# Regrouping the transposes and scores of a GLA and MLP layer, and cutting its first step by columns

## The chip, the cores and the metric

The kernel runs on one core of a Trainium2 chip. The metric is the device time of one execution, in microseconds (us). Before the change it is 1073.5 us, the median of three runs (1072.7, 1073.5 and 1073.9).

## The reference, cut to what matters

The layer takes 256 tokens of width 2048. It is a chunk-causal gated linear attention followed by a squared-ReLU MLP, each with a residual, and a final RMSNorm:

```
proj = rmsnorm(x) @ w_in              # q 1024, k 1024, v 2048, r 2048, g_low 16 columns
log_a = log_sigmoid(g_low @ w_gate_up + b_gate) / 16
# 4 heads, chunks of 64 tokens: the state decays per chunk, o = q_c @ state
h = x + (rmsnorm_per_head(o) * o_norm * silu(r)) @ w_out
a = relu(rmsnorm(h) @ w_up)           # 2048 -> 8192
h = h + (a * a) @ w_down              # 8192 -> 2048
out = rmsnorm(h)
```

Everything is float32 to the outside.

## The kernel before, in words

**Products.** A float32 product is made of three float32r matmuls. Each operand is split into a high part (rounded to float32r) and a low part (the rest), and the kernel adds high by high, high by low and low by high. `weights` (L119) loads a strip of 128 rows of a weight matrix with the SP queue into a `raw` buffer; `parts` (L105) makes the high part with a ScalarE cast (L109) and the low part with a VectorE subtraction (L110). There are five pairs of `hi`/`lo` buffers and six half buffers of `raw`, so casts run some steps ahead of TensorE. TensorE works with a stationary operand of 128x128 that is loaded anew for every matmul (the PEld rows) and a moving operand of 256 columns, or 272 in the first projection.

**Two forms of projection.** `natural` (L153) computes tokens by columns: 16 steps, one for each 128 rows (`kt`) of the contraction, each with 24 matmuls: two token tiles `t`, three terms, up to 1024 columns as halves of 256. The stationary operand is a row tile of activations given by the function `row`, the moving one the weights. `turned` (L168) computes columns by tokens, with the weights stationary: 16 values of `kt`, 12 matmuls each, loaded two `kt` at a time (`kp`). After each step (`natural`) or each `kt` (`turned`) but the last, `pump` (L88) takes one entry from the queue `side`; what is left at the end of a stage `flush` runs. So `side` spreads other work over the steps, and an entry `nothing` leaves a step empty. The position is not binding: the planner puts each instruction on its engine when its own timing model finds it ready, with the order of the program as the priority. Inside `pump`, `issue_after` only keeps an entry's ScalarE and VectorE work behind the latest cast.

**The stages, in order.** (1) The value and gate projection (`w_vg`, 1040 columns, L324). While it runs, `input_tile` (L248) loads x in six pieces and makes its high part `xh` (ScalarE, L255) and low part `xl` (VectorE, L256) for each `kt`; for the first three steps (`FINE`) the weights are loaded and cast in two pieces of columns. (2) The keys, two `turned` halves, with the gate's 22 entries in `side`, each followed by `nothing`: `turn_gate` (L343, two transposes), `gate_logits`, exponentials, scans. (3) The queries, two `turned` halves. (4) The second half of the values (`natural`, L480), with `scores` (L448): per head, three groups of plain float32 matmuls (12 records on TensorE) into two `aux` banks, evacuated by four ScalarE and four VectorE instructions. (5) The first half of the r projection (L533), with `attend`. (6) Its second half (L551), and (7), (8) the two halves of the output projection (L572, L579), with `turn` (L520): transposes of `on`, later of `h`, by plain float32 matmuls against `ident`, two `kt` (four transposes) at a time into one `aux` bank, then two ScalarE and two VectorE instructions that make the split parts. The last four of these calls run in the first `turned` stage of the MLP (`up`, L614), before the scale of the second norm (`scale2`, `scale2_row`). (9) Four rounds of `up` and `down`, and the end. PSUM is six `acc` banks and two `aux` banks.

**The operand at another address.** All stationary operands start 48 columns past a multiple of 64 columns (`OFF`). A few steps use one that starts at a multiple of 64 instead: `xe` (a copy of the row tile of `kt` 5, `t` 0, made in L260 and L261) in `row_x`; `row_o` for `kt` 5, `t` 0; and, in `turned`, the second `kt` of the pairs listed in `even`. `even_at` (L148) moves step `EVEN` (5) to another place in the order. These steps are called resets below.

**What follows a stage.** `put_v` (L317), `gate_out` (L512) and `add_h` (L559) read the four `acc` banks of a finished `natural`, two column halves `c` for each of two token tiles `t`, with `t` as the outer loop.

Of the kernel before, what the change touches and what calls it, by code (L numbers as in the profile page):

```python
# [32 lines left out]
P = 128  # L33
T = 256
# [32 lines left out]
def tile_gla_mlp(ctx, tc, x, xt, cols, w_vg, w_in, w_gate, w_out, w_up, w_down, final_norm, out):  # L67
# [14 lines left out]
    def aux_bank():  # L82
        return aux_p.tile([P, 512], F32, tag="aux", name="aux")
# [21 lines left out]
    def parts(raw, n, to, pieces=None):  # L105

        hi, lo = to
        for s in (slice(*p) for p in pieces or [(0, n)]):
            last_hi[0] = nc.scalar.copy(hi[:, s], raw[:, s])  # L109
            last_lo[0] = nc.vector.tensor_tensor(lo[:, s], raw[:, s], hi[:, s].bitcast(F32), op=ALU.subtract)  # L110
        return hi, lo
# [7 lines left out]
    def weights(src, n, pieces=None, room=None, skip=0, raw=None, gap=None):  # L119


        to = room or slots()
        if raw is None:
            if not raw_half:
                raw_half.extend(raw_pair())
            raw = raw_half.pop(0)
        for s in (slice(*p) for p in pieces or [(0, n)]):
            dst = raw[:, s]
            if len(src.shape) == 3:
                dst = dst.rearrange("p (i c) -> p i c", i=2)  # L130
                last_load[0] = nc.sync.dma_start(out=dst, in_=src)
                between = SLOT - OFF - 2 * GT if gap else 0
                to = [a[:, OFF - between : OFF + 2 * GT + between].rearrange("p (i c) -> p i c", i=2)[:, :, between:] for a in to]
                last_hi[0] = nc.scalar.copy(to[0], dst)  # L134
                last_lo[0] = nc.vector.tensor_tensor(to[1], dst, to[0].bitcast(F32), op=ALU.subtract)  # L135
                return to
            else:
                last_load[0] = nc.sync.dma_start(out=dst, in_=src[:, s])  # L138
        return parts(raw, n, to, pieces or [(skip, n)])

    def halves(o, x, w, first, last):

# [10 lines left out]
    def natural(row, source, n, cuts, pumps=1, ahead=None, order=range(KT)):  # L153

        acc = acc_banks(NT * len(cuts))
        acc = [acc[t * len(cuts) : (t + 1) * len(cuts)] for t in range(NT)]
        for step, kt in enumerate(order):
            wh, wl = weights(source(kt), n, ahead and ahead(kt))
            for t in range(NT):
                sh, sl = row(kt, t)  # L160
                for i, (s, w) in enumerate(((sh, wh), (sh, wl), (sl, wh))):
                    for c, (lo, hi) in enumerate(cuts):
                        halves(acc[t][c], s, w[:, lo:hi], step == 0 and i == 0, step == KT - 1 and i == 2)
            if step < KT - 1:
                pump(pumps)
        return acc
# [23 lines left out]
    def rows(w, c0, n=G, r0=0):  # L190
        return lambda kt: w[r0 + kt * P : r0 + (kt + 1) * P, c0 : c0 + n]
# [31 lines left out]

    xe = mid.tile([P, 2, P], F32R, tag="xe", name="xe")

    def row_x(kt, t):
        if kt == EVEN and t == 0:
            return [xe[:, i] for i in range(2)]
        return [a[:, kt, t * P : (t + 1) * P] for a in (xth, xtl)]

    def wrap_input(lo, hi):
        k = slice(lo, hi)
# [15 lines left out]
    def input_tile(kt):  # L248
        if kt in x_loads:
            s = slice(x_done[0], x_loads[kt])  # L250
            nc.sync.dma_start(out=xr[:, s, :], in_=xv[:, s, :])  # L251
            x_done[0] = x_loads[kt]
        if kt == KT - 1:
            wrap_input(0, KT - 2)
        nc.scalar.activation(xth[:, kt, :T], xr[:, kt, :], AF.Copy, scale=g1(kt))  # L255
        nc.vector.scalar_tensor_tensor(  # L256
            xtl[:, kt, :T], xr[:, kt, :], g1(kt), xth[:, kt, :T].bitcast(F32), op0=ALU.mult, op1=ALU.subtract
        )
        if kt == EVEN:
            nc.scalar.copy(xe[:, 0], xth[:, kt, :P].bitcast(F32))  # L260
            nc.vector.tensor_copy(xe[:, 1], xtl[:, kt, :P].bitcast(F32))  # L261
        return [(0, 512), (512, WMAX)] if kt < FINE else None


    h = const.tile([P, NT, D], F32, name="h")

    GR = 64 + RANK
# [53 lines left out]
            vh[:, t, c0 : c0 + n].bitcast(F32), op0=ALU.mult, op1=ALU.subtract,  # L321
        )

    acc = natural(row_x, rows(w_vg, 0, WMAX), WMAX, cuts, ahead=input_tile)  # L324
    flush()
    wrap_input(KT - 2, KT)
    for t in range(NT):
# [76 lines left out]
    gate += [lambda c=c: gate_scan(c) for c in range(8)]  # L404
    gate += [lambda i=i: gate_spans(i) for i in range(2)]
    gate += [gate_spans_even, gate_decays, gate_decays_even]
    for g in gate:
        side.extend([g, nothing])

# [5 lines left out]
        nc.vector.tensor_tensor(kab[:, 0, c], kab[:, 0, c], zz[:, 1, c], op=ALU.mult)  # L415

    for half in range(2):
        acc = turned(*xts, w_in, KEYW + half * GT, even=(0,) if half else (2,), acc=None if half else [aux_bank(), aux_bank()])
        for b in range(2):
            c0 = 4 * half + 2 * b  # L420
            from_bank(kab[:, 0, c0 : c0 + 2], acc[b])
# [88 lines left out]
    oth = otl = None  # L510

    def gate_out(acc, c0):  # L512
        for t in range(NT):
            for c in range(2):
                lo = c0 + 512 * c
                s = tmp.tile([P, 512], F32, tag="t512", name="sr", bufs=3)
                nc.scalar.activation(s, acc[t][c], AF.Silu, scale=r1[:, t : t + 1])
                nc.vector.tensor_tensor(on[:, t, lo : lo + 512], on[:, t, lo : lo + 512], s, op=ALU.mult)

    def turn(src, row, gain, q):  # L520
        b = aux_bank()
        for i in range(2):
            kt = 2 * q + i
            for t in range(NT):
                nc.tensor.transpose(b[:, i * T + t * P : i * T + (t + 1) * P], src[:, t, kt * P : (kt + 1) * P], ident)  # L525
        for i in range(2):
            kt = 2 * q + i
            s = b[:, i * T : (i + 1) * T].rearrange("p (t s) -> p t s", t=NT)
# [30 lines left out]
    def add_h(acc, c0):  # L559
        for t in range(NT):  # L560
            for c in range(2):
# [258 lines left out]
```

## Time and profile before

| what | value |
|---|---|
| median of three runs | 1073.5 us (1072.7 to 1073.9) |
| the profiled execution's own time | 1072.98 us |
| its span, first to last instruction | 1071.1 us |
| TensorE (PE) busy | 1061.8 us, 99%, 9283 matmul records |
| VectorE (DVE) busy | 775.1 us, 72% |
| ScalarE (ACT) busy | 574.2 us, 54% |
| GpSimd (POOL) busy | 12.7 us, 1% |
| read from HBM | 206.92 MB, 195 GB/s over the span |

The profile is one execution taken by the hardware profiler. PE rows are matmuls, PEld rows the loads of the stationary operand, which overlap them. Matmuls are pipelined, so a record is longer than the distance between the starts of two neighbours; that distance (the pitch) is what TensorE's time consists of, and it is read from the start times in the timeline. A row of a timeline holds its start, its length, the engine and line, the operation with the tiles it writes and reads, the shape and the number of records in it. What stands in brackets is idle time before it and who ended it.

### The profile page before, as it was taken

The page shows a single profiled execution, that of the slowest core. Times are in us where ns is not written, and L with a number is a line of the kernel's source. Part 1 is how long each engine was busy: PE and PEld are TensorE (multiplying, and loading weights), DVE is VectorE, ACT ScalarE, POOL GpSimd, SP SyncE. Part 2 cuts the span into 40 slices and gives each one's busy share as a digit, 9 for nine tenths or more (in the row PEclk, how much of TensorE's full clock was granted, in tenths as well). Part 3 has the DMA queues.
Part 4 walks back from the last instruction along what each step waited for, and adds up shares of the span by engine and source line. Part 5 has one row for each costly group of instructions (what it writes and reads, how often), then busy time and mean ns, then how long its engine had stood idle before and what let it go on. Part 6 is the DMA issues. An engine that isn't in the chain of part 4 may idle for free.

```text
span 1071.1 us, 21851 instructions
## 1 busy us (share of the span) xinstructions
PE 1061.8 (99%) x9283; PEld 1060.9 (99%) x9283; DVE 775.1 (72%) x1026; ACT 574.2 (54%) x693; POOL 12.7 (1%) x39
## 2 busy tenths in 40 slices
PE   9999999999999999999999999999999999999997
PEld 9999999999999999999999999999999999999997
DVE  7677654656555566789986689987779997678874
ACT  7675444546445455555555446564555554555552
POOL 0000000000000000000000000000000000000000
PEclk9999999999999999999999999999999999999999
DMA  9847654655555555555576555566655656665662
GB/s 341 305 157 233 196 185 137 178 151 179 197 183 183 186 179 183 194 190 201 197 227 204 191 194 173 195 223 210 197 197 179 213 200 215 191 194 189 205 228 79
DMA packets 79569, 210.43 MB, mean 196 GB/s; under 512 B 6720, under 2 KB 7616, under 8 KB 79344
## 3 DMA queue, kind: packets, MB, share of 16 engines
q1 hardware_dynamic: 78512, 206.99, 58.6%
q10 hardware_dynamic: 960, 2.05, 0.5%
q8 instruction: 72, 1.18, 0.4%
q14 instruction: 25, 0.20, 0.1%
HBM read 206.92 MB, written 2.10 MB: 195 GB/s over the span
## 4 chain that ended last, share of the span: by engine, by line
PE 96%; DMA 1%; issue 1%; ACT 0%; DVE 0%; SPq 0%; POOLq 0%; POOL 0%; DVEq 0%; ACTq 0%
PE acc L146 42%; PE acc L180 39%; PE aux L146 12%; PE aux L180 2%; DMA zz<-in_xt 1%; PE aux L525 1%; PE aux L454 1%; DMA raw<-in_w_vg 0%; ACT xh L255 0%; SPq L138 0%; DVE lo L110 0%; ACT hi L109 0%; PE acc L355 0%; SPq L251 0%; DVE hf L779 0%
## 5 line engine op out<-in xcount | busy, mean ns | idle before, releaser
L110 DVE TENSOR_TENSOR lo<-raw,hi 128x1024 fp32r<-128x1024 f32 (+2 forms) x225 | 258.5, 1151 | 123.2 <-ACT hi L109 122.2
L109 ACT CAST hi<-raw 128x1024 fp32r<-128x1024 f32 (+2 forms) x225 | 223.4, 994 | 214.9 <-PE acc L146 115.5
L180 PE MATMUL acc<-hh,hi 128*128 128x256 f32 x1024 | 283.2, 277 | 0.0
L180 PE MATMUL acc<-hh,lo 128*128 128x256 f32 x1024 | 283.1, 276 | 0.0
L180 PE MATMUL acc<-hl,hi 128*128 128x256 f32 x1024 | 283.0, 276 | 0.0
L135 DVE TENSOR_TENSOR lo<-raw,hi 128x1024 fp32r<-128x1024 f32 x160 | 195.7, 1224 | 115.3 <-ACT hi L134 114.6
L134 ACT CAST hi<-raw 128x1024 fp32r<-128x1024 f32 x160 | 168.1, 1051 | 187.5 <-PE acc L180 144.7
L146 PE MATMUL acc<-hi,act 128*128 128x256 f32 x1202 | 217.3, 276 | 0.0
L180 PEld LDWEIGHTS acc<-hh,hi 128*128 128x128 f32 x1024 | 192.3, 188 | 0.0
L180 PEld LDWEIGHTS acc<-hh,lo 128*128 128x128 f32 x1024 | 192.3, 188 | 0.0
L180 PEld LDWEIGHTS acc<-hl,hi 128*128 128x128 f32 x1024 | 192.3, 188 | 0.0
L146 PEld LDWEIGHTS acc<-hi,act 128*128 128x128 f32 x1202 | 180.2, 188 | 0.0
L146 PE MATMUL acc<-lo,act 128*128 128x256 f32 x601 | 142.1, 276 | 0.0
L146 PE MATMUL aux<-hi,act 128*128 128x256 f32 x716 | 135.1, 276 | 0.0
L146 PEld LDWEIGHTS aux<-hi,act 128*128 128x128 f32 x716 | 107.9, 188 | 0.0
L146 PEld LDWEIGHTS acc<-lo,act 128*128 128x128 f32 x601 | 101.9, 188 | 0.0
L146 PE MATMUL acc<-lo,xh 128*128 128x256 f32 x496 | 79.7, 279 | 0.1
L146 PE MATMUL acc<-hi,xh 128*128 128x256 f32 x496 | 78.7, 281 | 0.3 <-ACT hi L109 0.3
L146 PE MATMUL acc<-hi,xl 128*128 128x256 f32 x496 | 78.8, 278 | 0.0
L146 PE MATMUL aux<-lo,act 128*128 128x256 f32 x358 | 76.9, 276 | 0.0
L109 ACT CAST hi<-work 128x1024 fp32r<-128x1024 f32 x49 | 51.7, 1055 | 32.0 <-PE aux L146 12.0
L146 PEld LDWEIGHTS acc<-hi,xh 128*128 128x128 f32 x496 | 66.7, 188 | 0.8 <-ACT hi L109 0.7
(147 smaller groups left out, 1386.1 us busy)
## 6 DMA issues: line engine op xcount, KB each, us to landing
raw<-in_w_up SPq DMA_DIRECT2D x128, 512.0 KB, 4.5
raw<-in_w_down SPq DMA_DIRECT2D x128, 512.0 KB, 4.4
raw<-in_w_in SPq DMA_DIRECT2D x80, 512.0 KB, 4.6
raw<-in_w_out SPq DMA_DIRECT2D x32, 512.0 KB, 4.3
raw<-in_w_vg SPq DMA_DIRECT2D x13, 520.0 KB, 8.0
h<-in_x SPq DMA_DIRECT2D x4, 512.0 KB, 7.1
zz<-in_xt SPq DMA_DIRECT2D x3, 384.0 KB, 7.5
fb<-in_final_norm ACTq DMA_DIRECT2D x1, 1024.0 KB, 7.0
```

The lines of the kernel that those rows point to most:

```text
L109: last_hi[0] = nc.scalar.copy(hi[:, s], raw[:, s])
L110: last_lo[0] = nc.vector.tensor_tensor(lo[:, s], raw[:, s], hi[:, s].bitcast(F32), op=ALU.subtract)
L134: last_hi[0] = nc.scalar.copy(to[0], dst)
L135: last_lo[0] = nc.vector.tensor_tensor(to[1], dst, to[0].bitcast(F32), op=ALU.subtract)
L146: nc.tensor.matmul(o[:, m], x, w[:, m], start=first and c == 0, stop=last, skip_group_check=True)
L180: nc.tensor.matmul(o, u[:, i, s], m[:, kt], start=kt == 0 and n == 0 and j % 2 == 0, stop=kt == KT - 1 and n == 2, skip_group_check=True,)
L454: nc.tensor.matmul(o, kab[:, k[0], c0 + c, k[1] : k[1] + P], q(qt[:, c0 + c]), start=c == 0, stop=c == 1)
L525: nc.tensor.transpose(b[:, i * T + t * P : i * T + (t + 1) * P], src[:, t, kt * P : (kt + 1) * P], ident)
```

## The change

It makes these edits.

- `turn` handles four `kt` (eight transposes) into two `aux` banks in a call. `turns` puts two such calls into a stage, each after an entry `nothing`: after steps 1 and 3 of stages 6, 7 and 8; in the first `up` stage each entry has one more `nothing` behind it.
- `scores` entries get a `nothing` after each and three instead of one ahead; the gate's entries get five `nothing` ahead. Counting the queue through the stages, the four heads come after steps 8, 10, 12 and 14 of stage 4 (before: after 5, 6, 7 and 8), and `turn_gate` after `kt` 5 of the keys (before: after `kt` 0).
- Both value projections take `plain_x`, without the reset; the second one has the plain order of steps.
- Resets in `turned` move: the first half of the keys from pair 2 to pair 4, the first `up` from pair 5 to pair 6.
- In the first step of the first projection the products go by pieces of columns: for each of 512, 256 and 272 columns first high by high for both token tiles, then high weights by low x, then low weights by high x. The weights of the first two `kt` (before: three) are loaded in two pieces and cast in three.
- From `kt` 3 on, the split of x (`split_input`) is kept behind the casts of the previous step's weights, on ScalarE and on VectorE.
- `gate_out` and `add_h` go over columns first, then token tiles.

```diff
-        for s in (slice(*p) for p in pieces or [(0, n)]):
+        loads, pieces = pieces or ([(0, n)], [(skip, n)])
+        for s in (slice(*p) for p in loads):
...
-        return parts(raw, n, to, pieces or [(skip, n)])
+        return parts(raw, n, to, pieces)
...
+            terms = lambda t: [(row(kt, t)[x], (wh, wl)[y]) for x, y in ((0, 0), (0, 1), (1, 0))]
+            if ahead and step == 0:
+                for c, (lo, hi) in enumerate(cuts):
+                    for i in (0, 2, 1):
+                        for t in range(NT):
+                            s, w = terms(t)[i]
+                            halves(acc[t][c], s, w[:, lo:hi], i == 0, False)
+            else:
...
+    def plain_x(kt, t):
+        return [a[:, kt, t * P : (t + 1) * P] for a in (xth, xtl)]
...
+        with ExitStack() as order:
+            if kt >= FINE:
+                order.enter_context(tc.issue_after(last_hi[0].ins))
+                order.enter_context(tc.issue_after(last_lo[0].ins))
+            split_input(kt)
+        return ([(0, 512), (512, WMAX)], [(0, 256), (256, 512), (512, WMAX)]) if kt < 2 else None
...
-        return [(0, 512), (512, WMAX)] if kt < FINE else None
...
-    acc = natural(row_x, rows(w_vg, 0, WMAX), WMAX, cuts, ahead=input_tile)
+    acc = natural(plain_x, rows(w_vg, 0, WMAX), WMAX, cuts, ahead=input_tile)
...
+    side.extend([nothing] * 5)
     for g in gate:
         side.extend([g, nothing])
...
-        acc = turned(*xts, w_in, KEYW + half * GT, even=(0,) if half else (2,), acc=None if half else [aux_bank(), aux_bank()])
+        acc = turned(*xts, w_in, KEYW + half * GT, even=(0,) if half else (4,), acc=None if half else [aux_bank(), aux_bank()])
...
-    side.extend([lambda: None] + [lambda hd=hd: scores(hd) for hd in range(HEADS)])
-    acc = natural(row_x, rows(w_in, 3 * KEYW), G, HALF, order=even_at(11))
+    side.extend([nothing] * 3 + [f for hd in range(HEADS) for f in (lambda hd=hd: scores(hd), nothing)])
+    acc = natural(plain_x, rows(w_in, 3 * KEYW), G, HALF)
...
-        for t in range(NT):
-            for c in range(2):
+        for c in range(2):
+            for t in range(NT):
...
     def turn(src, row, gain, q):
-        b = aux_bank()
-        for i in range(2):
-            kt = 2 * q + i
+        bs = [aux_bank(), aux_bank()]
+        for i in range(4):
+            kt, b, o = 4 * q + i, bs[i // 2], i % 2 * T
             for t in range(NT):
-                nc.tensor.transpose(b[:, i * T + t * P : i * T + (t + 1) * P], src[:, t, kt * P : (kt + 1) * P], ident)
+                nc.tensor.transpose(b[:, o + t * P : o + (t + 1) * P], src[:, t, kt * P : (kt + 1) * P], ident)
...
-    side.extend([lambda: None] + [lambda q=q: turn(on, turned_o, gain_o, q) for q in range(4)])
+    def turns(src, row, gain, q0):
+        return [f for q in (q0, q0 + 1) for f in (nothing, lambda q=q: turn(src, row, gain, q))]
+    side.extend(turns(on, turned_o, gain_o, 0))
...
-    side.extend([lambda q=q: turn(on, turned_o, gain_o, q) for q in range(4, 8)])
+    side.extend(turns(on, turned_o, gain_o, 2))
...
-    side.extend([lambda: None] + [lambda q=q: turn(h, turned_h, g2, q) for q in range(4)])
+    side.extend(turns(h, turned_h, g2, 0))
...
-    side.extend([lambda q=q: turn(h, turned_h, g2, q) for q in range(4, 8)])
+    side.extend([f for g in turns(h, turned_h, g2, 2) for f in (g, nothing)])
...
-        acc = turned(hth, htl, w_up, r * D + q * GT, even=() if q > 1 or r > 0 and q else (5,) if r == q == 0 else (0,))
+        acc = turned(hth, htl, w_up, r * D + q * GT, even=() if q > 1 or r > 0 and q else (6,) if r == q == 0 else (0,))
```

More of the change, by code (lines that the diff above doesn't have):

```diff
@@ L158, in natural @@
             wh, wl = weights(source(kt), n, ahead and ahead(kt))
-            for t in range(NT):
[L160 to L163, printed above, removed]
+            terms = lambda t: [(row(kt, t)[x], (wh, wl)[y]) for x, y in ((0, 0), (0, 1), (1, 0))]
[7 more added lines that the diff above has]
+                for t in range(NT):
+                    for i, (s, w) in enumerate(terms(t)):
+                        for c, (lo, hi) in enumerate(cuts):
+                            halves(acc[t][c], s, w[:, lo:hi], step == 0 and i == 0, step == KT - 1 and i == 2)
             if step < KT - 1:
@@ L224, in tile_gla_mlp @@
     xe = mid.tile([P, 2, P], F32R, tag="xe", name="xe")
+    def plain_x(kt, t):
+        return [a[:, kt, t * P : (t + 1) * P] for a in (xth, xtl)]
     def row_x(kt, t):
-        if kt == EVEN and t == 0:
-            return [xe[:, i] for i in range(2)]
-        return [a[:, kt, t * P : (t + 1) * P] for a in (xth, xtl)]
+        return [xe[:, i] for i in range(2)] if (kt, t) == (EVEN, 0) else plain_x(kt, t)
     def wrap_input(lo, hi):
@@ L252, in input_tile, with split_input @@
             x_done[0] = x_loads[kt]
+        with ExitStack() as order:
[4 more added lines that the diff above has]
+        return ([(0, 512), (512, WMAX)], [(0, 256), (256, 512), (512, WMAX)]) if kt < 2 else None
+    def split_input(kt):
         if kt == KT - 1:
@@ L512, in gate_out @@
     def gate_out(acc, c0):
-        for t in range(NT):
-            for c in range(2):
+        for c in range(2):
+            for t in range(NT):
                 lo = c0 + 512 * c
@@ L520, in turn @@
     def turn(src, row, gain, q):
-        b = aux_bank()
-        for i in range(2):
-            kt = 2 * q + i
+        bs = [aux_bank(), aux_bank()]
+        for i in range(4):
+            kt, b, o = 4 * q + i, bs[i // 2], i % 2 * T
             for t in range(NT):
-                nc.tensor.transpose(b[:, i * T + t * P : i * T + (t + 1) * P], src[:, t, kt * P : (kt + 1) * P], ident)
-        for i in range(2):
-            kt = 2 * q + i
-            s = b[:, i * T : (i + 1) * T].rearrange("p (t s) -> p t s", t=NT)
+                nc.tensor.transpose(b[:, o + t * P : o + (t + 1) * P], src[:, t, kt * P : (kt + 1) * P], ident)
+        for i in range(4):
+            kt, b, o = 4 * q + i, bs[i // 2], i % 2 * T
+            s = b[:, o : o + T].rearrange("p (t s) -> p t s", t=NT)
             dh, dl = row(kt)
@@ L553, in tile_gla_mlp @@
     gate_out(acc, G)
-    side.extend([lambda q=q: turn(on, turned_o, gain_o, q) for q in range(4, 8)])
+    side.extend(turns(on, turned_o, gain_o, 2))
     hs = const.tile([P, NT, 4], F32, name="hs")
     def add_h(acc, c0):
-        for t in range(NT):
-            for c in range(2):
+        for c in range(2):
+            for t in range(NT):
                 lo = c0 + 512 * c
```

## The prediction

> **What bounds the kernel now.** I read the page first (busy shares, then the chain that ended last), then TensorE's timeline step by step, then ScalarE's where TensorE idles. From the page:
>
> ```profile
> PE 1061.8 (99%) x9283; PEld 1060.9 (99%) x9283; DVE 775.1 (72%) x1026; ACT 574.2 (54%) x693; POOL 12.7 (1%) x39
> PE 96%; DMA 1%; issue 1%; ACT 0%; DVE 0%; SPq 0%; POOLq 0%; POOL 0%; DVEq 0%; ACTq 0%
> ```
>
> TensorE bounds it nearly everywhere, so a gain must come from its idle time or its pitch. The pitch has two values. By the windows, 4412 records take 500 us between 560 and 1060 us: 113.3 ns each. Around the scores and the next stage's reset TensorE's timeline (start, length, what, records) shows:
>
> ```profile
> 156.22 0.62 PE L146 MATMUL acc<-lo,xh 128*128 128x256 f32 x4
> 156.68 0.62 PE L146 MATMUL acc<-hi,xl 128*128 128x256 f32 x4
> 157.13 1.70 PE L454 MATMUL aux<-qt,kab 128*128 128x128 f32 x12
> 158.59 0.72 PE L146 MATMUL acc<-hi,xh 128*128 128x256 f32 x4
> 159.15 0.63 PE L146 MATMUL acc<-lo,xh 128*128 128x256 f32 x4
> 159.62 0.63 PE L146 MATMUL acc<-hi,xl 128*128 128x256 f32 x4
> ...
> 186.41 0.63 PE L146 MATMUL acc<-lo,xh 128*128 128x256 f32 x4
> ...
> 191.12 0.63 PE L146 MATMUL acc<-hi,xl 128*128 128x256 f32 x4
> 191.59 0.64 PE L146 MATMUL acc<-hi,xe 128*128 128x256 f32 x4
> ...
> 193.02 0.62 PE L146 MATMUL acc<-hi,xh 128*128 128x256 f32 x4
> ```
>
> Four matmuls take 0.455 us before the group of scores and 0.47 us after it: from 186.41 to 191.12 us 40 take 4.71 us, 117.7 ns each. The reset (`xe`, 12 matmuls in 1.43 us) ends that, and the next stage runs at 113.3. The reset of this stage itself, at 177.43 us, was followed by 117.7 as before. So a plain float32 group costs 4.4 ns on every matmul up to the next reset that works. Of seven resets met in the slow state, five worked (59.5, 191.6, 259, 350.8, 398 us) and two didn't (20.1 and 177.4, in the two value projections). Once, at 298.4 us, a group of transposes itself brought 113.3 back.
>
> The start, where TensorE waits:
>
> ```profile
> 4.69 0.80 PE L146 MATMUL acc<-hi,xh 128*128 128x256 f32 x2
> 5.77 0.54 PE L146 MATMUL acc<-hi,xh 128*128 128x256 f32 x2 [0.28 <-ACT hi L109]
> 6.14 0.40 PE L146 MATMUL acc<-lo,xh 128*128 128x256 f32 x2
> ...
> 8.54 1.12 PE L146 MATMUL acc<-hi,xh 128*128 128x256 f32 x8
> ```
>
> The first step's 24 matmuls last from 4.69 to 8.54 us, 3.85 us, where step 1 needs 2.86. Its second pair waits for the second piece of weights, cast at 5.09. Then, around 23 us, from ScalarE and TensorE:
>
> ```profile
> 18.77 2.91 ACT L255 ACTIVATE xh<-zz,colt 128x256 fp32r<-128x256 f32 x7 [2.68 <-DMA zz<-in_xt]
> 21.86 1.06 ACT L109 CAST hi<-raw 128x1040 fp32r<-128x1040 f32 x1
> ...
> 22.97 1.22 PE L146 MATMUL acc<-hi,xh 128*128 128x256 f32 x8
> 24.25 0.75 PE L146 MATMUL acc<-lo,xh 128*128 128x256 f32 x4
> ```
>
> Seven splits of x, for steps 9 to 15, run ahead of the cast of step 6's weights, which had landed at 20.09 us. Four pitches there are too long: 45, 102, 219 and 106 ns, 0.47 us in all.
>
> **The change part by part.** The profiled execution took 1072.98 us (span 1071.1 and 1.9 around it), 0.5 below the median of 1073.5; the sum is made against 1072.98, and the 0.5 is added at the end.
>
> *First step by columns.* A 512-column cast takes 0.62 us; 256-wide splits follow each other every 0.40. So the first piece is ready about 0.2 us earlier and TensorE starts at 4.49. From the first 512 columns it now has 12 matmuls (`xl` ready at 4.54, both `lo` pieces by 5.5) before it needs the cast that ends at 5.72. But until about 6 us it isn't at full speed: the warm-up records stand 213 ns apart, the transposes of the same 128 columns later 109. At some 230 ns a matmul (between those 213 and the 254 read at 5.77) about 7 instead of 3 have begun by 6.03. I take 4 x 0.118 = 0.47 us gained. Ends: 1.0 gained, since step 1 can start no sooner than 7.5 (its weights are cast from 7.08); 0.3 lost, if the new order waits for a `lo` piece. By the Trainium skill ("TensorE: Matmul & The Clock Gate", section "What's actually happening") the clock opens after a free-running window of about 3.4 us of work. By that rule it could open anywhere from 4.5 to 7.9 us, and I estimate 1.05 to 0.37 us for this step; the trace agrees: the full pitch is read from 6.03 us, 5.0 us after the first matmul.
>
> *Loads of the third `kt` in one piece.* One SP issue fewer (0.43 us) and one cast fewer on each engine; the whole 520 KB must land (9.22 us) before the 1.06 us cast, ending at 10.3, with `lo` at 11.5. Step 2 starts near 10.95 and wants `lo` near 11.4: 0 to 0.15 us lost; I take 0, as the planner already moves ready products ahead.
>
> *Splits of x behind the casts.* From `kt` 3 each split waits for the previous step's cast; step `kt` needs its own cast anyway, which comes later. Per step ScalarE has 0.4 + 1.06 and VectorE 0.4 + 1.24 us of work in 2.88. Step 6's cast can then run at 20.1 to 21.2 and its `lo` to 22.4, for a step that starts at 22.5; step 7's weights land at 22.19 and are ready at 24.5, for 25.4. Gain 0.47; ends 0 and 0.47, nothing else stood there. ScalarE's block on the three `wgu` issues up to 18.73 us stays.
>
> *Keys.* `turn_gate` comes after `kt` 5 and the reset at `kt` 9 instead of 5: 48 matmuls more at 4.4 ns, 0.21 lost. The gate's later entries move five `kt`; they feed VectorE and ScalarE work needed two stages later. If this reset fails, the next is eight `kt` on: 0.4.
>
> *Second values.* The scores start after step 8 instead of 5: 72 matmuls leave the slow pitch, 0.32 gained; the lost reset didn't work and its 12 matmuls ran at 120: 0.03 gained. The last head now sits one step before the end, so its evacuation (2.9 us for head 0) stands before `put_v`. The next stage needs its third bank 1.4 us after it starts; before, that bank was free 1.1 us earlier: 0 to 0.3 lost, I take 0.
>
> *Transposes.* Their number stays. A group of four costs 445 ns beside its neighbours, so about 111 each; only the edge is saved when two groups merge, 9 ns: 0.07 in all. In stages 6 and 8 the slow stretch is as before (from after step 1 to step 5). In stage 7 it begins a step later but lacks the lucky return at 298.4: 84 instead of 64 matmuls, 0.09 lost. In `up` it is `kt` 3 to 13 instead of 1 to 11: nothing. The two banks of one call are evacuated while the stage runs (see the rivals). `gate_out` and `add_h`: the banks that the next stage needs first, 1.4 us after its start, are still read among the first two or three: nothing.
>
> Sum: -0.47 - 0.47 + 0.21 - 0.35 - 0.07 + 0.09 = -1.06 us: 1071.9, and 1072.4 beside the median.
>
> The resets rest on a pitch that depends on where the stationary operand starts. The Trainium skill speaks against it ("TensorE: Matmul & The Clock Gate", section "Step-by-step: what each phase is for"): loading the next weights doesn't steal read bandwidth from the running matmul. By that rule the moves of groups and resets would be worth nothing and the sum -1.0. The trace disagrees: same shapes, 113.3, 117.7 and 119 ns.
>
> **The rivals.**
>
> - *A, the start gives less.* The first step stays bound by its data and the stall reappears one step later: -0.2 in place of -0.94, 1073.1. For it: loads land one after another up to 18 us with the DMA engines fully busy. Against: the cast of step 6 waited for ScalarE, not for its load.
> - *B, a reset fails.* Dearest is the one at the start of the r projection, now only one step behind a group; 177.43 failed 6 matmuls behind one. Then that stage and five steps of the next, 21 x 24 matmuls, run at 117.7: 2.2 us, 1074.6. A failure at step 5 of stages 6 to 8 costs about 13 steps: 1.4, 1073.8. For it: two of seven failed. Against: the reset at the same place worked.
> - *C, a group brings the fast pitch back*, as at 298.4, in two of the five stretches: with 4 steps each some 0.4, or 0.7 in the values; or resets as before and the start's upper end (0.5 more): 1070.9. For it: one case in some eighteen groups. Against: all the others.
> - *D, the other side: the second turn of a stage comes too late.* A call now holds both banks. Before, two `kt` took from 249.14 to 252.71 us to evacuate, as ScalarE and VectorE alternate on one bank with a cast between: 3.6, so up to 7.1 for four, while the next call is due 5.6 after the transposes: 1.5 us late. That is inside step 4, ahead of the reset. From 2.8 us late on, it falls behind the reset of step 5, and 13 steps of the next stretch run slow: 1.4 us in each of three stages, 4.2 in all, 1076.6. If TensorE waits instead, 1.5 in each of four stages: 1078. Against: the two banks can be evacuated side by side, four pairs of 0.47 + 0.48 being 3.8.
> - *E, nothing moves*: the splits weren't the cause and the step is clock-bound: 1073.5 with the phase terms.
>
> **How the numbers follow.** Forecast 0.47 (own range 1071.4 to 1073.2), A and E 0.13, B 0.15, C 0.13, D 0.12. The bound for a change that can be told from none, about 0.2%, lies at 1071.35 and 1075.65. Forecast, A, E and B are inside, less some 0.02 of the forecast that falls below, and some 0.01 of B, two failures, above: same 0.72. C gives faster 0.15 with that rest; D and double failures slower 0.13. The range runs from C's middle (1070.6, the start's upper end with it) to 1075.5, which takes in all but half of C and D.
>
> **What would show it.** The first step shorter than 3.6 us, from about 4.5; splits of x and casts alternating on ScalarE up to 20 us, and no pitch over 150 ns at 22 to 25; the slow pitch from 66 us back instead of 61, and in the values only from 165; eight transposes as one row of 0.9 us; the fast pitch after each reset. Wrong would be: 117.7 lasting past a reset by a stage (B), idle time ahead of transposes or transposes after step 5 (D), or 113.3 right after a group (C).

## The result, and the profile after

The changed kernel takes 1075.39 us, the median of 20 executions (1074.87 to 1075.91), against 1073.16 for the kernel before in the same comparison (20 executions, 1072.56 to 1074.88). The ratio is 1.0019, with a 95% interval of 1.0013 to 1.0025: 2.2 us slower. The forecast was 1.1 us faster than the 1073.5 shown. The executions of the kernel before lie in two clusters (over all comparisons of this document 95 of 118 below 1074.0 and 23 between 1074.1 and 1075.1), which is why its range is so wide.

The profiled execution of the changed kernel took 1075.38 us, with a span of 1073.2 (1071.1 before). On its page the busy line of section 1 and the chain that ended last read:

```profile
PE 1064.2 (99%) x9283; PEld 1063.6 (99%) x9283; DVE 774.9 (72%) x1027; ACT 574.4 (54%) x694; POOL 12.8 (1%) x39
...
PE 98%; issue 1%; DMA 0%; SPq 0%; DVE 0%; ACT 0%; POOLq 0%; POOL 0%; DVEq 0%
```

TensorE has the same 9283 matmuls and is busy 2.4 us longer, and its share of the chain rose from 96% to 98% as that of DMA fell from 1% to 0%. So waits went away, and the matmuls themselves became slower. Where that happened is seen by the start of each stage's first matmul in the two traces:

| stage | before, us | after, us | difference | forecast |
|---|---|---|---|---|
| start and first projection (to its end) | 52.19 | 51.35 | -0.84 | -0.94 |
| keys, first half | 23.26 | 23.83 | +0.57 | +0.21 |
| keys, second half, and queries | 65.36 | 65.40 | +0.04 | 0 |
| second values (4) | 50.78 | 50.44 | -0.34 | -0.35 |
| r, first half (5) | 51.75 | 51.75 | 0 | 0 |
| r, second half (6) | 45.67 | 46.81 | +1.14 | -0.02 |
| output, first half (7) | 45.59 | 45.87 | +0.28 | +0.07 |
| output, second half (8) | 45.68 | 46.80 | +1.12 | -0.02 |
| first `up` | 24.57 | 24.72 | +0.15 | -0.02 |
| the rest, to the end | 666.20 | 666.26 | +0.06 | 0 |
| sum | 1071.06 | 1073.24 | +2.18 | -1.06 |

(The -0.07 for the edges of groups stands here divided over the four stages, and rounded.) Nearly the whole loss sits in stages 6 and 8. The view by windows shows it as fewer matmuls begun in the same time. Its columns are the window, its length, and then busy time and records of PE, PEld, DVE, ACT and POOL, TensorE's granted clock, the DMA share and GB/s. The kernel before:

```profile
248.00:300.00 52.00, 52.00 (x457) 52.00 (x456) 29.84 (x35) 26.75 (x35) 0.00 (x0) 1.00 0.56 183
335.00:380.00 45.00, 45.00 (x396) 45.00 (x396) 24.64 (x29) 22.32 (x33) 0.00 (x0) 1.00 0.56 188
```

The changed kernel:

```profile
60.00:74.00 14.00, 14.00 (x121) 14.00 (x119) 8.15 (x11) 8.17 (x13) 0.00 (x0) 1.00 0.57 192
248.00:300.00 52.00, 52.00 (x445) 52.00 (x444) 29.11 (x34) 25.93 (x34) 0.00 (x0) 1.00 0.57 183
335.00:380.00 45.00, 45.00 (x387) 45.00 (x386) 24.30 (x27) 21.77 (x32) 0.00 (x0) 1.00 0.54 182
```

TensorE is busy for the whole of each window and has the full granted clock (1.00), in both kernels, yet it begins 12 and 9 matmuls fewer in the last two (the kernel before has 126 in the first window, 5 more). Times 113 ns that is 1.4, 1.0 and 0.6 us. In the timeline of the changed kernel (start, length, engine and line, operation and tiles, shape, records) stage 6 shows why:

```profile
254.76 1.04 PE L541 MATMUL aux<-ident,on 128*128 128x128 f32 x8
...
258.46 0.65 PE L147 MATMUL acc<-hi,xe 128*128 128x256 f32 x4
...
259.90 0.63 PE L147 MATMUL acc<-hi,xh 128*128 128x256 f32 x4
260.38 0.63 PE L147 MATMUL acc<-lo,xh 128*128 128x256 f32 x4
260.85 0.63 PE L147 MATMUL acc<-hi,xl 128*128 128x256 f32 x4
```

Eight transposes, one step (24 matmuls) without side work, then the reset (`xe`, three rows, of which the first is shown). Behind it the rows start 0.47 to 0.48 us apart, that is 117.7 ns per matmul, as ahead of it: this reset fails. In the kernel before, the last group of this stage (four transposes) lay inside the reset, behind its first matmul:

```profile
258.59 0.28 PE L146 MATMUL acc<-hi,xe 128*128 128x256 f32 x1
258.71 0.60 PE L525 MATMUL aux<-ident,on 128*128 128x128 f32 x4
259.06 0.60 PE L146 MATMUL acc<-hi,xe 128*128 128x256 f32 x3
```

In stage 8 it lay behind the reset's second matmul (350.09, in a reset from 349.85). Both resets worked there. So the resets of stages 6 and 8 kept their step, but the last group moved from inside the reset to 24 matmuls ahead of it.

In the changed kernel the slow pitch lasts through stage 6 into stage 7, whose own reset, with the same eight transposes at the same distance, works:

```profile
305.47 0.64 PE L147 MATMUL acc<-hi,oth 128*128 128x256 f32 x4
...
306.90 0.62 PE L147 MATMUL acc<-hi,oth 128*128 128x256 f32 x4
307.35 0.62 PE L147 MATMUL acc<-lo,oth 128*128 128x256 f32 x4
```

From 306.90 on four matmuls take 0.45. In stage 8 the reset at 351.13 fails like that of stage 6, and the slow pitch lasts until the reset of the first `up` stage. In the keys the reset at `kt` 9 fails too; the gate's matmuls (L369) lie inside it and, two more at 65.97, right behind it:

```profile
65.01 0.40 PE L369 MATMUL acc<-gt,wgs 80*128 80x256 f32 x2
```

What was forecast for the start and the values is there. ScalarE alternates between splits of x and casts near 20 us, and the cast of step 6's weights, at 21.86 before, now waits for its load alone:

```profile
20.41 1.06 ACT L109 CAST hi<-raw 128x1040 fp32r<-128x1040 f32 x1 [0.91 <-DMA raw<-in_w_vg]
```

So TensorE no longer stalls at 22 to 25 us; four matmuls take 0.48 there, two rows of which are:

```profile
22.57 1.12 PE L147 MATMUL acc<-hi,xh 128*128 128x256 f32 x8
23.53 0.64 PE L147 MATMUL acc<-lo,xh 128*128 128x256 f32 x4
```

And the last scores, at 186.66 one step ahead of the next stage's reset at 191.02, did that reset no harm; behind it four matmuls take 0.46:

```profile
192.45 0.62 PE L147 MATMUL acc<-hi,xh 128*128 128x256 f32 x4
192.91 0.62 PE L147 MATMUL acc<-lo,xh 128*128 128x256 f32 x4
```

### The profile page after: what moved, and what is told of

Read it like the earlier page. It is cut to its first block, busy times and chain, and to the rows that moved or that the text cites. A ratio compares the mean times of both kernels' runs of the same rounds, so it can differ in the third digit from the quotient of the medians.

```text
span 1073.2 us, 21853 instructions
## 1 busy us (share of the span) xinstructions
PE 1064.2 (99%) x9283; PEld 1063.6 (99%) x9283; DVE 774.9 (72%) x1027; ACT 574.4 (54%) x694; POOL 12.8 (1%) x39
## 4 chain that ended last, share of the span: by engine, by line
PE 98%; issue 1%; DMA 0%; SPq 0%; DVE 0%; ACT 0%; POOLq 0%; POOL 0%; DVEq 0%
PE acc L147 43%; PE acc L188 39%; PE aux L147 12%; PE aux L188 2%; PE aux L541 1%; PE aux L469 1%; DMA raw<-in_w_vg 0%; SPq L139 0%; PE acc L369 0%; SPq L260 0%; DVE hf L798 0%; ACT sqf L751 0%; DVE h L658 0%; ACT hi L109 0%; POOLq L835 0%
## 5 line engine op out<-in xcount | busy, mean ns | idle before, releaser
L110 DVE TENSOR_TENSOR lo<-raw,hi 128x1024 fp32r<-128x1024 f32 (+3 forms) x226 | 258.8, 1147 | 131.3 <-ACT hi L109 130.3
L109 ACT CAST hi<-raw 128x1024 fp32r<-128x1024 f32 (+3 forms) x226 | 223.3, 990 | 226.9 <-PE acc L147 128.1
L147 PEld LDWEIGHTS acc<-lo,xh 128*128 128x128 f32 x504 | 68.1, 188 | 0.0
```

What stands on the lines that cost most here:

```text
L147: nc.tensor.matmul(o[:, m], x, w[:, m], start=first and c == 0, stop=last, skip_group_check=True)
```

## The experiments

The first theory is rival B of the prediction: the start and the scores gained what was forecast, and the loss is that resets fail. What makes them fail was open: how the groups lie (theory 1), what came before (rival 2), their nearness (rival 3). Each kernel below was timed against the kernel before on the same chip; a profile of each gives the lengths of the stages.

**One part undone or alone.** Two kernels keep one part alone, and two put one back.

`start_alone`, the kernel before with the hunks of `weights`, of `natural`'s first step and of `input_tile`:

```diff
+            if ahead and step == 0:
+                for c, (lo, hi) in enumerate(cuts):
...
+            split_input(kt)
+        return ([(0, 512), (512, WMAX)], [(0, 256), (256, 512), (512, WMAX)]) if kt < 2 else None
...
```

> Edit: the kernel before with the edits of the start alone (first step by pieces of columns, third weights in one piece, splits of x behind the casts). Theory 1 (the start gained what the trace shows and the loss lies only in resets that fail): the second stage begins 0.84 us earlier than before, every later stage keeps its length, 1072.3 against 1073.2. Rival (the gain is given back later, because weights or buffers are late where TensorE is ahead): between 1073.0 and 1073.4, with some later stage longer by as much.

Measured: 1072.90 against 1073.20, ratio 0.9995 (0.9987 to 1.0004). The keys begin at 51.83 instead of 52.19, only 0.36 earlier, and their first half takes 23.81 instead of 23.26: their reset, at its old place, fails here. All later stages keep their length within 0.07. The expected 1072.3 is missed by that failure, and the time alone can't be told from that of the kernel before. So no wait for data gives the start back later, but the outcome of a reset that no edit touched has changed. Its surroundings did change: the gate's transposes, at 57.73 and 59.26 ahead of the reset (from 59.48) in the kernel before, lie inside it here (59.50 and 60.20, in a reset from 58.91 to 60.43). Why the start itself gained less than in the changed kernel is told below.

`four`, the changed kernel with the transposes as before:

```diff
-    side.extend(turns(on, turned_o, gain_o, 0))
+    side.extend([lambda: None] + [lambda q=q: turn(on, turned_o, gain_o, q) for q in range(4)])
...
-        bs = [aux_bank(), aux_bank()]
-        for i in range(4):
+        b = aux_bank()
+        for i in range(2):
...
```

> Edit: the changed kernel with the old calls of four transposes, each after steps 1 to 4 (0 to 3 in stage 7), the old reset of the first up stage and the old loop order behind a stage. Theory 1 (how the groups lie decides whether the reset at step 5 works): the resets at about 258 and 350 us work again, stages 6 and 8 are 1.1 us shorter each, stage 7 0.3 shorter: 1072.9 against 1075.4 for the changed kernel. Rival 2 (what the scores or the start left behind decides it): both resets still fail, 1075.2 or so.

Measured: 1072.43, ratio 0.9990 (0.9981 to 0.9999), 2.96 below the changed kernel. Stages 6, 7 and 8 take 45.47, 45.59 and 45.68. In stage 6 the second group of four itself brings the fast pitch back, which is rival C, one time in this stage:

```profile
251.76 0.60 PE L540 MATMUL aux<-ident,on 128*128 128x128 f32 x4
...
252.66 0.62 PE L147 MATMUL acc<-lo,xh 128*128 128x256 f32 x4
253.11 0.62 PE L147 MATMUL acc<-hi,xl 128*128 128x256 f32 x4
```

So the calls of the transposes (or the loop order and the reset of `up` that go back with them) carry the loss; the start and the scores, still in this kernel, don't.

`keys_back`, the changed kernel with the old place of the gate's entries and of the keys' reset:

```diff
-    side.extend([nothing] * 5)
...
-        acc = turned(*xts, w_in, KEYW + half * GT, even=(0,) if half else (4,), ...
+        acc = turned(*xts, w_in, KEYW + half * GT, even=(0,) if half else (2,), ...
```

> Edit: the changed kernel with the gate's entries and the reset of the first half of the keys back where they were (transposes after the first kt, reset in the third pair). Theory 1 (the reset at kt 9 failed, and the slow pitch lasted a stage): first half of the keys 23.3 instead of 23.8 us, 1074.85. Rival (the half is longer because of something else, such as the gate's work in it): no shorter, 1075.4.

Measured: 1073.59, 1.80 below the changed kernel, not 0.55. The first half of the keys takes 23.25, as expected. But stage 6 is 45.67 as well: its reset works, almost 200 us after that of the keys, with the same eight transposes at the same distance. (Without the five empty entries the queue runs ahead: the scores come a step earlier; `attend` lies where it did.) Stage 8 still fails, 46.80. So the outcome hangs on more than where the group lies.

`turns_alone`, the kernel before with the edits of `turn`, `turns`, the moved reset of `up` and the loop order:

```diff
-    side.extend([lambda: None] + [lambda q=q: turn(on, turned_o, gain_o, q) for q in range(4)])
+    side.extend(turns(on, turned_o, gain_o, 0))
...
-        acc = turned(hth, htl, w_up, ... else (5,) if r == q == 0 else (0,))
+        acc = turned(hth, htl, w_up, ... else (6,) if r == q == 0 else (0,))
```

> Edit: the kernel before with the edits of the transposes alone (eight a call, two steps apart, the moved reset of the first up stage, the loop order behind a stage). Theory 1 (the loss sits in how these groups lie to the resets, and whether one fails hangs on what came before it): at least one of the resets at 258 and 350 us fails, 1.1 us or more lost, 1074.2 to 1075.4. Rival 2 (what the start and the scores left behind made them fail): neither fails, 1073.2.

Measured: 1074.59 against 1073.19, ratio 1.0013 (1.0004 to 1.0022): slower by 1.40. Stage 6 works (45.67), stage 8 fails (46.80), and the `up` stage behind it takes 24.72 instead of 24.57. By the stages this one failure costs 1.12 + 0.15 = 1.27, near the 1.4 at which the prediction priced it; stage 7 is 0.08 longer (45.67), as it lacks the lucky return, and the start of this execution 0.22.

**What the failing reset needs.** Six kernels keep all of the change and disturb one thing near the reset of step 5.

`one_more` and `two_more` put one or two matmuls with an all-zero moving operand ahead of the step, in stages 6 and 8; `one_more_stage7` puts one in stage 7 alone:

```diff
+            if kt == EVEN:
+                for _ in range(more):
+                    halves(acc[1][1][:, :T], row(kt, 1)[0], zero, False, False)
...
-    acc = natural(row_x, rows(w_in, 5 * KEYW), G, HALF)
+    acc = natural(row_x, rows(w_in, 5 * KEYW), G, HALF, more=1)
```

> Edit: the changed kernel with one more float32r matmul (an all-zero moving operand, so the sum stays the same) right ahead of the reset's step in stages 6 and 8. Theory 1a (the slow state has a phase that moves with every matmul, and the reset works from some of them): the resets at 258 and 350 us come out differently, that is they work: 1.1 us less in each stage, 0.24 for the two matmuls: 1073.1. Theory 1b (the phase is set by the groups alone and stays from one matmul to the next): the resets fail as before, 1075.6. A reset that works after one and fails after two would be 1a.

> Edit: as with one extra all-zero matmul ahead of the reset's step in stages 6 and 8, but two. Theory 1a with a phase that alternates from one matmul to the next: both resets fail as without any, stages 6 and 8 of 47.05 us, 1075.6. Theory 1a with a longer period, or a rival in which any interruption of the step order heals the reset: both work, stages of 45.9, 1073.2.

> Edit: the changed kernel with one extra all-zero matmul ahead of the reset's step in stage 7 alone, where the reset works without it; there the first matmul after the last transposes took 202 ns, where the resets failed 204 and 205. Theory 1a (the extra matmul moves the phase): this reset fails now, stage 7 is about 46.9 us instead of 45.9. Rival (an extra matmul only ever helps): stage 7 keeps 45.9 plus 0.12.

Measured: 1072.92 with one and 1073.19 with two. More work makes the kernel 2.5 and 2.2 us faster. Stages 6 and 8 take 45.80 and 45.79 with one, 45.91 and 45.89 with two: about 0.12 for each extra matmul, and the resets work. In `one_more`:

```profile
258.12 0.28 PE L147 MATMUL acc<-zero,xh 128*128 128x256 f32 x1
258.24 0.64 PE L147 MATMUL acc<-hi,xe 128*128 128x256 f32 x4
...
259.67 0.62 PE L147 MATMUL acc<-hi,xh 128*128 128x256 f32 x4
260.12 0.62 PE L147 MATMUL acc<-lo,xh 128*128 128x256 f32 x4
```

Up to 258.12 this is the failing stage 6 of the changed kernel, pitch for pitch to 1 ns; four matmuls take 0.45 behind the reset instead of 0.47. In `one_more_stage7` (1075.47) stage 7 keeps its outcome: 45.99, that is 45.87 plus 0.12. So a phase that alternates from one matmul to the next (the short form of theory 1a) is out: one and two heal alike, and one where nothing is wrong doesn't spoil it. A phase with a long period isn't excluded. The simpler reading that is left is that something out of the ordinary right ahead of the reset heals it.

`split_one` tests whether the all-zero operand did it, with real operands only: the last matmul ahead of the step is cut in two.

```diff
+                            if split and (kt, t, i, c) == (EVEN - 1, 1, 2, 1):
+                                for m in (slice(0, T), slice(T, T + P), slice(T + P, 2 * T)):
+                                    halves(acc[t][c][:, m], s, w[:, lo:hi][:, m], False, False)
...
```

> Edit: the changed kernel with the last matmul ahead of the reset's step, in stages 6 and 8, cut into two of 128 columns: no operand that was not there, no more columns, one record more. Theory 1a (the rhythm in which the loads and the matmuls meet is what counts): the resets work, stages 6 and 8 of about 45.8 us, 1073.0. Rival 4 (the all-zero operand healed it by where it lies): they fail as before, 1075.4.

Measured: 1072.98; stages 6 and 8 take 45.67 and 45.66. In the timeline five records stand where four stood, the first row of the reset lasts 0.53 instead of 0.48, and the fast pitch follows:

```profile
258.37 0.69 PE L147 MATMUL acc<-hi,xl 128*128 128x256 f32 x5
258.89 0.69 PE L147 MATMUL acc<-hi,xe 128*128 128x256 f32 x4
...
260.37 0.62 PE L147 MATMUL acc<-hi,xh 128*128 128x256 f32 x4
260.83 0.39 PE L147 MATMUL acc<-lo,xh 128*128 128x256 f32 x2
```

So it isn't the all-zero operand; one matmul in two pieces ahead of the reset is enough, and costs nothing that can be measured here.

`reset_later` and `group_at_reset` move the two apart or together:

```diff
-    acc = natural(row_x, rows(w_in, 5 * KEYW), G, HALF)
+    acc = natural(row_x, rows(w_in, 5 * KEYW), G, HALF, order=even_at(7))
...
```

```diff
-        return [f for q in (q0, q0 + 1) for f in (nothing, lambda q=q: turn(src, row, gain, q))]
+        return [nothing, lambda: turn(src, row, gain, q0), nothing, nothing, lambda: turn(src, row, gain, q0 + 1)]
...
```

> Edit: the changed kernel with the reset's step two places later (after step 6) in stages 6 and 8, so that 72 instead of 24 matmuls lie between the last transposes and the reset. Theory 1a (phase; 48 more is a multiple of any short period): the resets fail as before, 1075.4. Rival 3 (the reset comes too soon after a group of eight): they work, stages 6 and 8 are shorter by 113.3 against 117.7 over the 8 to 9 steps left, 0.9 each, 1073.4.

> Edit: the changed kernel with the second eight transposes of stages 6, 7 and 8 after step 4 instead of 3, right ahead of the reset's step. Theory 1a: the reset starts from another phase in all three stages; where the first matmul behind the group takes 201 to 202 ns it works, where it takes 204 to 205 it may fail; no time can be told ahead, 1073.0 to 1075.4. Rival 5 (groups of eight spoil the reset wherever they lie): stages 6 and 8 stay at 46.8, 1075.4.

Measured: 1075.48 with the reset two steps later, stages of 46.81 and 46.80: 72 regular matmuls between group and reset instead of 24 change nothing, and the failing reset begins with the same pitches as in the changed kernel, 121, 120 and 124 ns. Rival 3 is out. With the group right ahead of the reset: 1072.81, and all three resets work (45.67, 45.67, 45.66). Groups of eight are no harm by themselves (rival 5 is out); where the last group lies to the reset matters, and this kernel puts it back about where the kernel before had it. The four kernels that healed both resets took 1072.41 to 1073.52 in all their executions, the changed kernel never less than 1074.87.

Over stages 6 to 8 of all kernels with eight transposes the trace has a sign that tells the outcome ahead. It is the distance from the start of the first matmul behind the last group to the next one, read from the start times of single records:

| first pitch behind the last group | what lies between it and the reset | resets that work |
|---|---|---|
| 201 to 202 ns | 24 regular matmuls | 9 of 9 |
| 204 to 205 ns | 24 or 72 regular matmuls | 0 of 8 |
| 202 to 205 ns | 24 matmuls, then an extra or a cut one | 7 of 7 |
| 201 or 204 ns | nothing | 3 of 3 |

So a plain float32 group leaves one of at least two slow states that look alike (117.7 ns), that stay as they are over 72 regular matmuls, and from one of which the reset doesn't lead out. This is one profile of each kernel, and the sign is shown for these stages only. What decides which state comes was not found: in stage 8 it is 204 to 205 in all eight kernels that keep the groups of eight at their new place, in stage 6 204 to 205 in six and 201 to 202 in `keys_back` and `turns_alone`. Those two are also the only ones of the nine whose keys' reset worked, which may be chance. What the state is inside TensorE stays open.

**A version from what was learnt.** `start_scores` keeps only the start and the scores. `four_keys` takes the changed kernel with the transposes by four and lets the keys' reset come at `kt` 7, ahead of the gate's matmuls:

```diff
-        acc = turned(*xts, w_in, KEYW + half * GT, even=(0,) if half else (4,), ...
+        acc = turned(*xts, w_in, KEYW + half * GT, even=(0,) if half else (3,), ...
```

> Edit: only the start and the second value projection as in the changed kernel; the gate's entries, the first resets of the keys and of the MLP, the transposes by four and the old loop order as before. Theory 1 (the gains of the two parts stand by themselves): 0.84 and 0.34 below the kernel before if the reset of the keys works, 1072.0; 0.55 more if it fails, 1072.5.

> Edit: the changed kernel with the transposes by four as before, and the reset of the first half of the keys one pair earlier than changed (kt 7, right behind the gate's transposes and ahead of the gate's other matmuls). Theory 1 (the reset of the keys failed since the gate's matmuls cut it in two): it works, the half takes 23.2 us instead of 23.8, 1071.9. Rival (it fails by its phase): 23.8, 1072.4 as with the transposes by four alone.

Measured: `start_scores` 1072.74 against 1073.09, ratio 0.9993 (0.9984 to 1.0002). The keys' reset at its old place failed again (23.81), the case forecast at 1072.5, with the gate's transposes inside it (59.09 and 59.79, in a reset from 58.49 to 60.01). In `keys_back` they lie there too, and TensorE's first 2084 matmuls, up to 244 us, are the same in the same order in both kernels; yet there the reset works (23.25). So TensorE's order of work alone doesn't settle the outcome, and what differs isn't seen in these two profiles. Nor does the sign of the table hold in the keys: the first pitch behind the last transposes is 201 ns where this reset failed and 202 where it worked. `four_keys` takes 1072.12 against 1073.19, ratio 0.9989 (0.9980 to 0.9998), and is the fastest of all. Its keys take 23.39 instead of 23.83, against 23.2 expected: here the reset works and the gate's matmuls come behind it, with 124 records in the window where the changed kernel has 121:

```profile
60.00:74.00 14.00, 14.00 (x124) 14.00 (x123) 8.19 (x11) 8.21 (x13) 0.00 (x0) 1.00 0.60 196
```

## Why the prediction was wrong, point by point

*First step by columns, -0.47: mis-sized.* Step 2 began at 11.05 us instead of 11.40 in the profiled executions, 0.35 earlier. Over the twelve profiles with the new start it began between 10.70 and 11.53, in the mean at 11.18, and in the two with the old start (the kernel before and `turns_alone`) at 11.40 and 11.14. So the term is about 0.1, not 0.47, as far as two profiles of the old start can tell. The step that failed is that I took the moment of full pitch, 6.03 us, as the kernel's, where it is the execution's. The changed kernel has it from its second matmul:

```profile
4.47 0.77 PE L147 MATMUL acc<-hi,xh 128*128 128x256 f32 x4
5.09 0.63 PE L147 MATMUL acc<-hi,xl 128*128 128x256 f32 x4
```

and then waits in step 1 (from 7.58) for weights, up to 0.3 us a time, which is the lower bound of 7.5 that the prediction gave. `start_alone`, with the same order of matmuls here, is at 213 ns until 7.2 us and has no wait after it:

```profile
4.48 1.20 PE L147 MATMUL acc<-hi,xh 128*128 128x256 f32 x4
5.48 1.05 PE L147 MATMUL acc<-hi,xl 128*128 128x256 f32 x4
```

Over all fourteen profiles the full pitch sets in between 4.0 and 7.2 us, 2.9 to 6.1 after the first warm-up record at 1.04, while the granted clock in the view by windows reads 1.00 throughout. The Trainium skill ("TensorE: Matmul & The Clock Gate", section "What's actually happening") has a free-running window of about 3.4 us; the spread of 3.2 us is near one such window, but the earliest, 2.9 us, is shorter than one, and the ±500 ns that the same section gives is far too small here. The prediction quoted the rule and its range and still took the one row for the sum.

*Third weights in one piece, 0:* right; step 2 lasts 2.88 us, as every later one.

*Splits of x behind the casts, -0.47: right in its mechanism.* Steps 2 to 12 take 2.88 us in all twelve profiles with the new start. With the old one steps 5 and 6 together cost 0.46 more in the kernel before and 0.94 more in `turns_alone`. So the two terms of the start share the gain differently from one execution to the next. Together they come near the forecast of 0.94: the first projection ends at 51.49 in the mean of the twelve, and at 52.30 in that of the two, 0.81 later.

*Keys, +0.21, or 0.4 more if the reset fails:* it failed, and 0.57 was lost; the unlikely branch at its price. The working left out that the gate's next entries, moved by the same five places, come to lie inside the reset. `four_keys`, whose reset lies ahead of those entries, fits that, but its reset is also nearer to the transposes. `start_alone` and `start_scores` fail at the old place and `keys_back` works there, so the cause in the keys stays open.

*Second values, -0.35:* -0.34, right, and the reset of the r projection one or two steps behind a group worked in every profile that has it, the place that rival B called the dearest.

*Transposes, -0.07 and +0.09: this is where the prediction fell.* "In stages 6 and 8 the slow stretch is as before (from after step 1 to step 5)" took the reset at step 5 as a thing that works where it had worked. But the group in front of it had moved: from inside the reset to 24 matmuls ahead of it. The reset failed in both: +1.14 and +1.12, with +0.28 and +0.15 in the stages behind them, 2.69 in all (0.08 of the 0.28 stands also where the reset of stage 6 works, and was forecast). Rival B had the mechanism and its price: 1.4 for such a failure, two of them 2.8; `turns_alone` shows one at 1.27 by its stages. What was wrong is its chance. All of B got 0.15, and two failures together 0.01, from the argument that "the reset at the same place worked", which holds for its step and not for what lies around it. (The prediction puts the two resets at 259 and 350.8, behind the group; they begin ahead of it, at 258.59 and 349.85.) The count in the same prediction, two of seven failed, was a reason to hold every moved group for a new draw: with four moved resets at two in seven each, none failing would have had a chance of some 0.26 (0.71 to the fourth), an estimate from that count alone.

*Waits (rival D) and the loop order:* none seen; the second transposes come after step 3 in each stage, and the stages behind `gate_out` and `add_h` begin without a gap. *Rival C* didn't come in the changed kernel, and did in stage 6 of `four`. *Rival A* was half right: step 1 is bound by its data when the full pitch sets in early.

The time lies inside the range given (1070.6 to 1075.5), at its upper edge, and this is owed to the width of the range and not to the sum. The profile is 3.24 us above the sum: 2.68 in the four stages with transposes, 0.36 in the keys, 0.10 in the start, and the rest small.

## What to carry to other kernels

Where a speed rests on a state of the engine that a special step restores, treat each edit that moves work ahead of that step as a new draw, and read the outcome in the trace at every such step; a place where it worked is no evidence for another order of work. Prefer an arrangement that doesn't hang on it: in stages 6 to 8 a float32 group directly ahead of the reset (3 of 3), or an irregular matmul there (7 of 7), went with a reset that works. In the keys, work inside the reset went both ways. And a start whose full pitch sets in at a different moment in each execution is judged by several profiles, not by one.

## What the runs showed of the hardware that was not expected

- An added matmul made the kernel 2.5 us faster (`one_more`), and a matmul cut into two halves 2.4 us (`split_one`): each let a reset work that had failed.
- Three pitches belong to the same matmul of 128x128 by 256 columns with a load for each, at a granted clock of 1.00: 113.3 ns, 117.7 and, on operands at the other address, 120. In stages 6 to 8 two slow states of 117.7 can be told apart ahead of the reset by the first matmul behind a float32 group (201 to 202 or 204 to 205 ns), and then by the reset's own first pitches (in the changed kernel 117, 118 and 120 ns in stage 7, where it works, and 121, 120 and 124 in stage 6, where it doesn't).
- An edit in the keys at 60 us, which also moved the scores by a step, changed the outcome of a reset at 258 us (`keys_back`), with the fast pitch of 113.3 for most of the time in between. Whether a difference that isn't seen in the pitch is carried through the fast state, or the order of the work on the way decides, or something outside TensorE's order, wasn't separated.
- Two kernels with the same TensorE work in the same order up to 244 us had the reset of the keys work in one and fail in the other (`keys_back`, `start_scores`).
- The distance of the two clusters of the kernel before, about 1.5 us, is near the price of one failed reset (1.4). No profile of the upper cluster was taken, so that this is its cause was only argued.
